# A different order of weight casts, evictions and sums where a kernel passes from plain products to block products

## The chip, the cores and the metric

One core of a Trainium2 chip runs the program. Its engines work side by side, each through a queue in program order: TensorE (PE; PEld is its weight load), VectorE (DVE), ScalarE (ACT), GpSimd (POOL) and SyncE (SP), which here only issues transfers. What counts is the device time of one execution in microseconds (us), as the median of several.

## The reference

The program computes one layer of a decoder for 512 prompt tokens and 32 sample tokens, 544 columns in all. The change lies in the first part of the feed-forward network:

```python
u = x * (1 + sc2) + sh2
h = (jax.nn.silu(u @ w_gate) * (u @ w_up)) @ w_down
x = layer_norm(DN_ALPHA * x + (1 + g2) * h, ln2_g, ln2_b)
```

`x` has 1024 channels; the hidden width is 2816, which makes 22 feature blocks of 128. Ahead of it stand the modulation, the input projection, convolution, attention, the output projection and the first layer norm, which the change leaves alone.

## The kernel before, in words

**Precision.** Each operand of a product is held as a rounded high part and a remainder. A weight tile of 128x1024 is loaded by SP into one of four raw buffers (`wr`), cast on ACT into a high part (`wh`, line 133), and DVE subtracts to get the remainder (`wl`, line 134). Three buffers each of `wh` and `wl` go round. Three products make one: high by high, high by remainder, remainder by high.

**Halves.** The 544 columns are two halves of 272. A group (`mm_group`, lines 199 to 202) multiplies one weight tile by both halves: 48 matmuls of 272 columns, into two of the four PSUM banks of `mm`. Two groups, gate and up of a feature block, are evicted together: a sigmoid on ACT and a multiply on DVE (lines 1050, 1052), a multiply by the up result (1057), a cast of the hidden value on ACT (1059) and its remainder on DVE (1061).

**The passage.** Feature blocks 0 and 1 are computed for the first half of the columns alone, then, once the layer norm of the second half is done, for the second half (lines 1307 to 1309, four other banks). So their four evictions of the first half (`first`) and of the second half (`second`) come apart. Feature blocks 2 and 3 are plain groups: gate 2, up 2, gate 3, up 3. Their weight tiles are here called by these names. Gate 2 has a buffer of its own; up 2, gate 3 and up 3 use the three round buffers, which the tiles of blocks 0 and 1 hold until the second half is done.

From block 4 on a block is computed by seven half-size products (`seven`, 12 matmuls each, 84 in all) instead of eight. The products are called by the operands of the weight: A11, S1, S2, S3, A12, A22, S4. The S operands are sums of quarter blocks: POOL makes them for the weights (line 1112, `add_up`), ACT and DVE cast and subtract them (`unit_high`, lines 1128 and 1139). The same kinds of sum of `u2`, the normed input, are made once, in the passage: ACT computes `u2` again unrounded into `tf` (line 1289, eight times), DVE makes four sums (1294, 1298 as `t3`, 1299, 1301 as `t4`), ACT casts them into `tb` and `ta` (1295, 1300, 1321, 1332) and DVE makes the remainders (1316, 1317, 1322, 1334). `ta` lies in the memory of `tf`, so its first cast waits until `tf` is read out. The weight sums `ss` lie in the memory of `t3`, so the first weight sum waits for line 1322, which reads `t3` last. A block's S4 sum overwrites its S1 sum, and the next block's S1 sum overwrites that.

**What sets the order.** Order on PE, ACT, DVE and POOL is written out by hand: an engine runs its instructions as the program text issues them, and waits where data or a buffer is not ready. `prep_to(n)` issues casts and remainders of weights up to number n, and with each a next load on SP; `w_next(k)` does so k ahead. The text of the passage is in the branch `if j == 0`.

## Time and profile before

| | us |
|---|---|
| median of 3 runs | 1026.58 (1026.53 to 1027.11) |
| the profiled execution | 1026.28 |
| its span on the chip | 1024.5 |
| the passage on PE, gate 2 to the end of up 3 | 645.06 to 678.37 |
| blocks 4 to 7 | 678.37 to 723.35 |

The granted TensorE clock was 0.993 over the span. Times in the time line count from the start of the span. A row of the time line gives the start, the length, the engine, the line, the operation and its tiles; in square brackets stands how long the engine had been idle and what ended that. In the tables a number behind x is a count of instructions. Buffer numbers are left out of names, so `wh` is any of the three.

### The profile page before, as it was taken

The numbers are of one execution on the slowest core, as the hardware profiler recorded it, in microseconds if no ns is written. First come the engines' busy times: TensorE is split into PE (matmuls) and PEld (weight loads), VectorE is DVE, ScalarE is ACT, GpSimd is POOL, SyncE is SP. The second block draws the span as 40 slices with busy tenths as digits, with TensorE's granted clock in tenths as the row PEclk, the third lists the DMA queues.
The fourth block names the chain that finished last, engine by engine and source line by source line (L and its number), as shares of the span: only waits on it lengthen the run. The fifth ranks groups of instructions, "written<-read, shape, count | busy, mean of one in ns | idle before, by whom it ended". The sixth has DMA issues, their size and how long they took to land.

```text
span 1024.5 us, 21678 instructions
## 1 busy us (share of the span) xinstructions
PE 989.5 (97%) x9000; PEld 945.6 (92%) x9000; DVE 649.0 (63%) x1165; ACT 492.5 (48%) x963; POOL 223.8 (22%) x266
## 2 busy tenths in 40 slices
PE   7999999999999999999999999899999999999994
PEld 6987899999988989999999998799999999999994
DVE  3523688879886554342216888688546875488687
ACT  3412335545447666534435745556435652356333
POOL 0201010010014310101103135054024430344046
PEclk9999999999999999999999999999999999999998
DMA  9998787796785574699943620125964769566612
GB/s 368 377 423 293 259 302 279 246 338 233 279 300 199 210 265 162 244 373 398 373 187 109 249 66 21 42 83 201 352 227 166 267 229 344 206 247 223 207 46 82
DMA packets 46529, 242.64 MB, mean 237 GB/s; under 512 B 7584, under 2 KB 12448, under 8 KB 39520
## 3 DMA queue, kind: packets, MB, share of 16 engines
q1 hardware_dynamic: 36896, 135.70, 36.8%
q10 hardware_dynamic: 7488, 87.95, 23.1%
q0 software_dynamic: 2048, 17.63, 4.4%
q8 instruction: 70, 1.15, 0.4%
q14 instruction: 27, 0.22, 0.1%
HBM read 231.36 MB, written 97.58 MB: 321 GB/s over the span
## 4 chain that ended last, share of the span: by engine, by line
PE 56%; DVE 13%; issue 10%; ACT 8%; DMA 7%; POOL 6%; ACTq 0%; SPq 0%; POOLq 0%; DVEq 0%
PE mm L199 13%; PE mm L200 13%; PE mm L202 13%; POOL ss L1112 4%; DMA gb<-in_w_ada 3%; DMA wr<-in_w_gu 2%; PE od L766 2%; PE mm L1155 2%; PE Sd L731 2%; PE mm L1157 2%; PE mm L1156 2%; DVE wl L134 1%; PE pt L542 1%; DMA wr<-in_w_in 1%; PE adaps L357 1%
## 5 line engine op out<-in xcount | busy, mean ns | idle before, releaser
L199 PE MATMUL mm<-u,wh 128*128 128x272 f32 x1016 | 284.2, 297 | 4.4 <-ACT wh L133 4.1
L200 PE MATMUL mm<-u,wh 128*128 128x272 f32 x1016 | 276.5, 290 | 0.0
L202 PE MATMUL mm<-u,wl 128*128 128x272 f32 x1016 | 213.4, 290 | 1.0 <-DVE wl L134 1.0
L199 PEld LDWEIGHTS mm<-u,wh 128*128 128x128 f32 x1016 | 192.9, 190 | 19.2 <-issue 9.8
L200 PEld LDWEIGHTS mm<-u,wh 128*128 128x128 f32 x1016 | 193.5, 190 | 0.2
L134 DVE TENSOR_TENSOR wl<-wr,wh 128x1024 fp32r<-128x1024 f32 (+2 forms) x97 | 117.2, 1209 | 82.3 <-ACT wh L133 81.3
L202 PEld LDWEIGHTS mm<-u,wl 128*128 128x128 f32 x1016 | 160.4, 189 | 1.4 <-DVE wl L134 1.4
L133 ACT CAST wh<-wr 128x1024 fp32r<-128x1024 f32 (+2 forms) x97 | 94.0, 970 | 48.5 <-PE mm L200 34.6
L465 DVE SCALAR_TENSOR_TENSOR convy<-glu,vec,convy 128x512 f32<-128x512 f32 x120 | 95.7, 797 | 2.5
L1112 POOL TENSOR_TENSOR ss<-wr 128x512 f32<-128x512 f32 x34 | 51.7, 1520 | 192.7 <-DVE s L1139 84.3
L200 PE MATMUL mm<-h,wh 128*128 128x272 f32 x240 | 64.8, 288 | 0.0
L199 PE MATMUL mm<-h,wh 128*128 128x272 f32 x240 | 64.5, 287 | 0.0
L1069 DVE SCALAR_TENSOR_TENSOR z<-mm,modT,z 128x272 f32<-128x272 f32 (+1 forms) x48 | 21.7, 479 | 50.9 <-PE mm L202 50.9
L663 ACT ACTIVATE qk<-mm,vec 128x272 f32<-128x272 f32 (+1 forms) x48 | 25.8, 624 | 53.9 <-PE mm L202 53.9
L202 PE MATMUL mm<-h,wl 128*128 128x272 f32 x240 | 49.7, 289 | 0.0
L1128 ACT CAST wh<-ss 128x512 fp32r<-128x512 f32 (+1 forms) x34 | 28.4, 835 | 42.8 <-POOL ss L1112 33.1
L199 PEld LDWEIGHTS mm<-h,wh 128*128 128x128 f32 x240 | 45.2, 188 | 0.0
L200 PEld LDWEIGHTS mm<-h,wh 128*128 128x128 f32 x240 | 45.2, 188 | 0.0
L535 ACT ACTIVATE P<-P,st 128x256 f32<-128x256 f32 x64 | 31.2, 488 | 28.3 <-DVE st L529 25.8
L1155 PE MATMUL mm<-ta,wh 128*128 128x272 f32 x136 | 40.5, 297 | 2.4 <-DVE wg L1177 2.4
L680 POOL DMA_DIRECT2D out_kv<-qk x4 | 2.4, 597 | 176.9 <-ACT qk L663 176.9
L1157 PE MATMUL mm<-tb,wl 128*128 128x272 f32 x136 | 39.5, 290 | 0.0
(342 smaller groups left out, 2547.6 us busy)
## 6 DMA issues: line engine op xcount, KB each, us to landing
out_s<-in_c ACTq DMA_DIRECT2D x32, 2044.0 KB, 9.6
wr<-in_w_in SPq DMA_DIRECT2D x57, 512.0 KB, 6.5
wr<-in_w_gu SPq DMA_DIRECT2D x44, 512.0 KB, 4.0
KT<-in_kt SPq DMA_DIRECT2D x24, 792.0 KB, 7.7
VV<-in_vv SPq DMA_DIRECT2D x24, 768.0 KB, 7.3
out_s<-in_c ACTq DMA_DIRECT2D x8, 2032.0 KB, 9.7
...
```

The source lines that it names most:

```text
L133: act.copy(out=hv, in_=raw)
L134: dve.tensor_tensor(out=lv, in0=raw, in1=hv.bitcast(F32), op=ALU.subtract)
L199: pe.matmul(ps[h][:, :HC], lhsT=hi[:, k], rhs=A[h][:, 0, k], start=(k == 0), stop=False)
L200: pe.matmul(ps[h][:, :HC], lhsT=hi[:, k], rhs=A[h][:, 1, k], start=False, stop=False)
L202: pe.matmul(ps[h][:, :HC], lhsT=lo[:, k], rhs=A[h][:, 0, k], start=False, stop=(k == nk - 1))
L465: dve.scalar_tensor_tensor(out=o, in0=src, scalar=sc, in1=o, op0=ALU.mult, op1=ALU.add)
L535: act.activation(out=p[:, a:b], in_=p[:, a:b], func=AF.Exp, bias=st[:, kd, s, hh, 0:1], accum_out=st[:, kd, s, hh, 1:2])
L663: act.activation(out=o, in_=src, func=AF.Identity, bias=V("b_in", col))
L1112: pool.tensor_tensor(out=o, in0=x, in1=y, op=op)
L1128: act.copy(out=hi, in_=src_of(f, n))
L1155: pe.matmul(ps[:, :HC], lhsT=hi[:, k], rhs=B[:, 0, k], start=(first and k == 0), stop=False, skip_group_check=not first)
L1157: pe.matmul(ps[:, :HC], lhsT=lo[:, k], rhs=B[:, 0, k], start=False, stop=(k == 3), skip_group_check=not first)
```

## The change

The four casts and remainders of up 2, gate 3, up 3 and of A11 of block 4 are issued at other places between the evictions and the `u2` sums. The second halves' sigmoids and multiplies are put ahead of their other eviction steps, in tiles of another tag. The four weight sums of block 4 are issued at the start of the passage and go to four tiles of their own (`early`); S2 and S3 of block 4 are therefore cast and subtracted one by one. PE, SP and POOL run the same instructions in the same order as before.

On ACT, at the start of the passage, before (`wr_7019` is up 2, `sgf_7581` the gate of feature block 1, first half, `tb` the `u2` sums):

```order
L1050 ACTIVATE sgf_7581<-mm_7510 128x272
L1059 CAST h00_7388<-sgf_7581 128x272
L1295 CAST tb_7564<-tf_7239 128x1088
L1289 ACTIVATE tf_7239<-z_6753,B9_6400,G9_6399 128x272 x4
L133 CAST wh_7593<-wr_7019 128x1024
L1300 CAST tb_7564<-tf_7239 128x1088
```

and in the change (`wg_7571` and `wg_7591` are the gates of feature blocks 0 and 1, `wr_7051` is gate 3):

```order
L1062 CAST h00_7388<-wg_7571 128x272
L133 CAST wh_7577<-wr_7019 128x1024
L1053 ACTIVATE wg_7591<-mm_7510 128x272
L1312 ACTIVATE tf_7239<-z_6753,B9_6400,G9_6399 128x272 x4
L1062 CAST h00_7388<-wg_7591 128x272
L133 CAST wh_7748<-wr_7051 128x1024
L1333 CAST tb_7564<-tf_7239 128x1088
```

Up 2 moved from behind the second eviction, the first `tb` cast and eight recomputations to right behind the first eviction; gate 3 stands ahead of the first `tb` cast.

On ACT, up 3 (`wr_7392`), before (`sgf_7761` and `sgf_7763` are gate 2, `wr_7051` gate 3):

```order
L1050 ACTIVATE sgf_7761<-mm_7699 128x272
L1050 ACTIVATE sgf_7763<-mm_7700 128x272
L133 CAST wh_7767<-wr_7051 128x1024
L1059 CAST h00_7388<-sgf_7761 128x272
L1059 CAST h01_7389<-sgf_7763 128x272
L1321 CAST ta_7831<-t3_7565 128x1088
L133 CAST wh_7838<-wr_7392 128x1024
```

and in the change (`wg_7755` and `wg_7757` are gate 2, `wg_7761` and `wg_7764` the second halves):

```order
L1053 ACTIVATE wg_7755<-mm_7697 128x272
L1053 ACTIVATE wg_7757<-mm_7698 128x272
L1053 ACTIVATE wg_7761<-mm_7560 128x272
L1053 ACTIVATE wg_7764<-mm_7562 128x272
L1312 ACTIVATE tf_7239<-z_6753,B9_6400,G9_6399 128x272 x4
L1062 CAST h01_7389<-wg_7761 128x272
L1062 CAST h01_7389<-wg_7764 128x272
L1341 CAST tb_7564<-tf_7239 128x1088
L133 CAST wh_7831<-wr_7392 128x1024
```

Up 3's cast no longer stands behind the eviction of feature block 2 and the cast of `ta`, but behind the second halves' evictions, four recomputations and the second `tb` cast.

On DVE, where the block products begin, before (`mm_7844` and `mm_7845` are gate 3, `mm_7910` and `mm_7911` up 3, `ss` the weight sums):

```order
L1322 TENSOR_TENSOR ta_7831<-t3_7565,ta_7831 128x1088
L134 TENSOR_TENSOR wl_7839<-wr_7392,wh_7838 128x1024
L1139 TENSOR_TENSOR wl_7895<-wr_7569,wh_7894 128x512
L1139 TENSOR_TENSOR wl_7895<-ss_7834,wh_7894 128x512
L1052 TENSOR_TENSOR sgf_7900<-sgf_7900,mm_7844 128x272
L1052 TENSOR_TENSOR sgf_7902<-sgf_7902,mm_7845 128x272
L1334 TENSOR_TENSOR ta_7831<-t4_7566,ta_7831 128x1088
L1139 TENSOR_TENSOR wl_7961<-ss_7834,wh_7960 128x1024
L1057 TENSOR_TENSOR sgf_7900<-sgf_7900,mm_7910 128x272
L1057 TENSOR_TENSOR sgf_7902<-sgf_7902,mm_7911 128x272
```

and in the change (`mm_7850` and `mm_7851` are gate 3, `mm_7912` and `mm_7913` up 3, `ss4` the weight sums of block 4):

```order
L1165 TENSOR_TENSOR wl_7847<-wr_7569,wh_7846 128x512
L1354 TENSOR_TENSOR ta_7845<-t3_7565,ta_7845 128x1088
L1165 TENSOR_TENSOR wl_7847<-ss4_7583,wh_7846 128x512
L1055 TENSOR_TENSOR wg_7905<-wg_7905,mm_7850 128x272
L1055 TENSOR_TENSOR wg_7907<-wg_7907,mm_7851 128x272
L1163 TENSOR_TENSOR wl_7963<-ss4_7585,wh_7962 128x512
L1163 TENSOR_TENSOR wl_7963<-ss4_7587,wh_7962 128x512
L1361 TENSOR_TENSOR ta_7845<-t4_7566,ta_7845 128x1088
L1060 TENSOR_TENSOR wg_7905<-wg_7905,mm_7912 128x272
L1060 TENSOR_TENSOR wg_7907<-wg_7907,mm_7913 128x272
```

The remainder of up 3 has left this piece for an earlier place, the A22 pass (line 1334, now 1361) went behind S2 and S3, and the weight sums come from tiles that do not wait for `t3`.

The diff:

```diff
@@ -1043,10 +1043,13 @@
         tick()
 
 
-    def gate_evict(pg):
+    def small(pool_, tag):
+        return pool_.tile([128, NT if tag == "w" else 512], F32, tag=tag, name="wg")[:, :HC]
+
+    def gate_evict(pg, tag="w"):
         sg = {}
         for h in pg:
-            sg[h] = tmp.tile([128, HC], F32, tag="w", name="sgf")
+            sg[h] = small(tmp, tag)
             act.activation(out=sg[h], in_=pg[h][:, :HC], func=AF.Sigmoid)
         for h in pg:
             dve.tensor_tensor(out=sg[h], in0=sg[h], in1=pg[h][:, :HC], op=ALU.mult)
@@ -1089,7 +1092,7 @@
 
 
     UNITS = ("A11", "S1", "S2", "S3", "A12", "A22", "S4")
-    rw, place, sums, T, own = {}, {}, set(), {}, {}
+    rw, place, sums, T, own, early = {}, {}, set(), {}, {}, {}
 
     def rhs_of(n):
         return T[n] if n in T else {"A11": u2[0][:, :, 0:4], "A12": u2[0][:, :, 4:8], "S4": u2[1][:, :, 4:8]}[n]
@@ -1102,6 +1105,17 @@
 
     def add_up(f, n):
         g, u = raw_of(f)
+        if f == 4:
+            e = early[f, n] = tmp4.tile([128, 4, 128], F32, tag="P", name="ss4")
+            x, y, op = {
+                "S1": (lambda: u[:, 0:4], lambda: u[:, 4:8], ALU.add),
+                "S2": (lambda: early[f, "S1"], lambda: g[:, 0:4], ALU.subtract),
+                "S3": (lambda: g[:, 0:4], lambda: u[:, 0:4], ALU.subtract),
+                "S4": (lambda: g[:, 4:8], lambda: early[f, "S2"], ALU.subtract),
+            }[n]
+            pool.tensor_tensor(out=e, in0=x(), in1=y(), op=op)
+            sums.add((f, n))
+            return
         SS = own["SS"]
         o, x, y, op = {
             "S1": (SS[:, 2], u[:, 0:4], u[:, 4:8], ALU.add),
@@ -1115,7 +1129,11 @@
     def src_of(f, n):
         g, u = raw_of(f)
         assert n[0] == "A" or (f, n) in sums
-        return {"A11": g[:, 0:4], "A12": g[:, 4:8], "A22": u[:, 4:8], "S1": own["SS"][:, 2], "S4": own["SS"][:, 2], "S2": own["SS"][:, 0:2]}[n]
+        if f == 4 and n[0] == "S":
+            return early[f, n]
+        if n[0] == "A":
+            return {"A11": g[:, 0:4], "A12": g[:, 4:8], "A22": u[:, 4:8]}[n]
+        return {"S1": own["SS"][:, 2], "S4": own["SS"][:, 2], "S2": own["SS"][:, 0:2]}[n]
 
     def unit_high(f, n, twice=False):
         j = UNITS.index(n)
@@ -1125,7 +1143,11 @@
             if j // 2 not in ring:
                 ring[j // 2] = (whp.tile([128, 8, 128], F32R, tag="wh", name="wh"), wlp.tile([128, 8, 128], F32R, tag="wl", name="wl"))
             hi, lo = (t[:, 4 * (j % 2):4 * (j % 2) + (8 if n == "S2" else 4)] for t in ring[j // 2])
-        act.copy(out=hi, in_=src_of(f, n))
+        if n == "S2" and f == 4:
+            for i, m in enumerate(("S2", "S3")):
+                act.copy(out=hi[:, 4 * i:4 * i + 4], in_=src_of(f, m))
+        else:
+            act.copy(out=hi, in_=src_of(f, n))
         if n == "S2":
             place[f, 2], place[f, 3] = (hi[:, 0:4], lo[:, 0:4]), (hi[:, 4:8], lo[:, 4:8])
         else:
@@ -1136,7 +1158,11 @@
             act.copy(out=seen, in_=f32(hi))
 
         def low():
-            dve.tensor_tensor(out=lo, in0=src_of(f, n), in1=seen, op=ALU.subtract)
+            if n == "S2" and f == 4:
+                for i, m in enumerate(("S2", "S3")):
+                    dve.tensor_tensor(out=lo[:, 4 * i:4 * i + 4], in0=src_of(f, m), in1=seen[:, 4 * i:4 * i + 4], op=ALU.subtract)
+            else:
+                dve.tensor_tensor(out=lo, in0=src_of(f, n), in1=seen, op=ALU.subtract)
             if n == "A22":
                 i = gu_at[2 * f]
                 done[i] = done[i + 1] = True
@@ -1155,9 +1181,6 @@
             pe.matmul(ps[:, :HC], lhsT=hi[:, k], rhs=B[:, 0, k], start=(first and k == 0), stop=False, skip_group_check=not first)
             pe.matmul(ps[:, :HC], lhsT=hi[:, k], rhs=B[:, 1, k], start=False, stop=False, skip_group_check=not first)
             pe.matmul(ps[:, :HC], lhsT=lo[:, k], rhs=B[:, 0, k], start=False, stop=(k == 3), skip_group_check=not first)
-
-    def small(pool_, tag):
-        return pool_.tile([128, NT if tag == "w" else 512], F32, tag=tag, name="wg")[:, :HC]
 
     rest = {}
 
@@ -1288,17 +1311,14 @@
                 for k in ks:
                     act.activation(out=tf[:, k // 4, k % 4], in_=z[:, k, :HC], func=AF.Identity, scale=G9[:, k, 0:1], bias=B9[:, k, 0:1])
 
+            f = 4
             gu_evict({0: first[0]}, {0: first[1]}, H, 0)
+            prep_to(pos["use"] + 2)
+            for n in ("S1", "S2", "S3", "S4"):
+                add_up(f, n)
+            sg = gate_evict({0: first[2]})
             again(range(4))
-            gu_evict({0: first[2]}, {0: first[3]}, H, 1)
-            dve.tensor_tensor(out=tf[:, 0], in0=tf[:, 2], in1=tf[:, 0], op=ALU.subtract)
-            act.copy(out=T["S1"][:, 0], in_=tf[:, 0])
-            again(range(4, 8))
-            prep_to(pos["use"] + 2)
-            dve.tensor_tensor(out=t3, in0=tf[:, 3], in1=tf[:, 2], op=ALU.subtract)
-            dve.tensor_tensor(out=tf[:, 3], in0=tf[:, 3], in1=tf[:, 0], op=ALU.subtract)
-            act.copy(out=T["S2"][:, 0], in_=tf[:, 3])
-            dve.tensor_tensor(out=t4, in0=tf[:, 1], in1=tf[:, 3], op=ALU.subtract)
+            up_evict(sg, {0: first[3]}, H, 1)
             A = u2[1]
             for k in range(8):
                 for i in range(4):
@@ -1308,33 +1328,38 @@
                     pe.matmul(ps, lhsT=lo[:, k], rhs=A[:, 0, k], start=False, stop=False)
                     pe.matmul(ps, lhsT=hi[:, k], rhs=A[:, 1, k], start=False, stop=(k == 7))
             pg = mm_group(w_next(2), u2, 8)
+            dve.tensor_tensor(out=tf[:, 0], in0=tf[:, 2], in1=tf[:, 0], op=ALU.subtract)
+            prep_to(pos["use"] + 2)
+            act.copy(out=T["S1"][:, 0], in_=tf[:, 0])
+            sg = gate_evict(pg)
+            sec = [gate_evict({1: second[2 * i]}, "PT") for i in range(2)]
+            again(range(4, 8))
             for i in range(2):
-                gu_evict({1: second[2 * i]}, {1: second[2 * i + 1]}, H, i)
-            sg = gate_evict(pg)
+                up_evict(sec[i], {1: second[2 * i + 1]}, H, i)
+            dve.tensor_tensor(out=t3, in0=tf[:, 3], in1=tf[:, 2], op=ALU.subtract)
+            dve.tensor_tensor(out=tf[:, 3], in0=tf[:, 3], in1=tf[:, 0], op=ALU.subtract)
+            act.copy(out=T["S2"][:, 0], in_=tf[:, 3])
+            dve.tensor_tensor(out=t4, in0=tf[:, 1], in1=tf[:, 3], op=ALU.subtract)
+            pu = mm_group(w_next(2), u2, 8)
             prep_to(pos["use"] + 2)
-            pu = mm_group(w_next(2), u2, 8)
+            up_evict(sg, pu, H, 2)
             dve.tensor_tensor(out=T["S1"][:, 1], in0=tf[:, 0], in1=f32(T["S1"][:, 0]), op=ALU.subtract)
             dve.tensor_tensor(out=T["S2"][:, 1], in0=tf[:, 3], in1=f32(T["S2"][:, 0]), op=ALU.subtract)
-            up_evict(sg, pu, H, 2)
             TA = big_tile(0, [128, 2, 2, 4, HC], F32R, "ta")
             T["S3"], T["A22"] = TA[:, 0], TA[:, 1]
+            unit_a = unit_high(f, "A11")
             act.copy(out=T["S3"][:, 0], in_=t3)
+            pg = mm_group(w_next(1), u2, 8)
+            unit_a()
             dve.tensor_tensor(out=T["S3"][:, 1], in0=t3, in1=f32(T["S3"][:, 0]), op=ALU.subtract)
             own["SS"] = one.tile([128, 3, 4, 128], F32, tag="vT", name="ss")
-            f = 4
-            for n in ("S1", "S2", "S3"):
-                add_up(f, n)
-            prep_to(pos["use"] + 2)
-            pg = mm_group(w_next(2), u2, 8)
-            unit(f, "A11")
             unit(f, "S1")
             sg = gate_evict(pg)
             act.copy(out=T["A22"][:, 0], in_=t4)
-            add_up(f, "S4")
+            pu = mm_group(w_next(1), u2, 8)
+            unit(f, "S2")
             dve.tensor_tensor(out=T["A22"][:, 1], in0=t4, in1=f32(T["A22"][:, 0]), op=ALU.subtract)
             own["S4"] = one.tile([128, 2, 4, 128], F32R, tag="osb", name="s4")
-            pu = mm_group(w_next(1), u2, 8)
-            unit(f, "S2")
             up_evict(sg, pu, H, 3)
             unit(f, "A12")
             rest["a22"] = unit_high(f, "A22")
```

## The prediction

> **What bounds the kernel now.** I read the page first, then the busy time in stretches around the place of the change, then the time line of TensorE (PE), VectorE (DVE), ScalarE (ACT) and GpSimd (POOL) there. The page says that PE has work nearly all the time:
>
> ```profile
> PE 989.5 (97%) x9000; PEld 945.6 (92%) x9000; DVE 649.0 (63%) x1165; ACT 492.5 (48%) x963; POOL 223.8 (22%) x266
> ```
>
> So a gain must come out of stretches in which PE waits or is slow. The table of stretches (start:end, length, busy time of PE, PEld, DVE, ACT, POOL with instruction counts, granted PE clock, DMA share, GB/s) is cut where each piece of the passage starts on PE: gate 2, up 2, gate 3, up 3, then the blocks 4, 5, 6 and 7 of seven products.
>
> ```profile
> 645.06:651.11 6.05, 6.05 (x50) 5.97 (x48) 2.52 (x4) 3.23 (x7) 0.00 (x0) 1.00 0.00 1
> 651.11:661.95 10.84, 8.06 (x50) 7.63 (x48) 7.12 (x9) 4.87 (x10) 0.00 (x0) 0.84 0.16 48
> 661.95:672.35 10.40, 8.07 (x51) 7.70 (x50) 8.96 (x13) 4.91 (x9) 1.25 (x1) 0.84 0.18 53
> 672.35:678.37 6.02, 6.02 (x51) 6.02 (x50) 5.89 (x6) 3.24 (x5) 5.94 (x4) 1.00 0.30 87
> 678.37:690.87 12.50, 10.85 (x87) 10.63 (x85) 9.60 (x16) 7.31 (x14) 6.07 (x5) 1.00 0.29 85
> 690.87:701.93 11.06, 10.84 (x86) 10.62 (x85) 8.68 (x18) 6.65 (x13) 5.47 (x4) 1.00 0.76 274
> 701.93:712.77 10.84, 10.84 (x87) 10.63 (x85) 8.65 (x18) 6.62 (x13) 5.47 (x4) 1.00 0.36 108
> 712.77:723.35 10.58, 10.58 (x86) 10.58 (x85) 8.63 (x17) 4.25 (x8) 0.00 (x0) 1.00 0.80 290
> ```
>
> Without a wait a group of 48 matmuls takes 6.05 us (0.126 each) and a block of 84 takes 10.58. Against that, up 2 loses 4.79, gate 3 4.35, block 4 1.92, block 5 0.48 and block 6 0.26: 11.80 us in all, which no reordering here can exceed. PE's own rows say what it waited for:
>
> ```profile
> 653.54 0.40 PE L199 MATMUL mm<-u,wh 128*128 128x272 f32 x1 [2.29 <-ACT wh L133]
> 654.80 0.52 PE L202 MATMUL mm<-u,wl 128*128 128x272 f32 x2 [0.49 <-DVE wl L134]
> 663.94 0.39 PE L199 MATMUL mm<-u,wh 128*128 128x272 f32 x1 [1.83 <-ACT wh L133]
> 665.20 0.65 PE L202 MATMUL mm<-u,wl 128*128 128x272 f32 x2 [0.49 <-DVE wl L134]
> 687.75 0.39 PE L1155 MATMUL mm<-ta,wh 128*128 128x272 f32 x1 [1.65 <-DVE wg L1177]
> ```
>
> In both weight stages PE waits for the rounding cast on ACT (wh) and then for its remainder on DVE (wl): 2.78 and 2.32 us. What is left of 4.79 and 4.35, 2.0 each, is the clock: it was 0.84 in both stretches. Why is up 2's cast late? It is not the transfer:
>
> ```profile
> 649.42 1.10 ACT L1295 CAST tb<-tf 128x1088 fp32r<-128x1088 f32 x1 [1.77 <-DVE tf L1294]
> 650.43 2.12 ACT L1289 ACTIVATE tf<-z,B,G 128x272 f32<-128x272 f32 x4
> 652.46 1.03 ACT L133 CAST wh<-wr 128x1024 fp32r<-128x1024 f32 x1
> 653.52 1.23 DVE L134 TENSOR_TENSOR wl<-wr,wh 128x1024 fp32r<-128x1024 f32 x1 [4.19 <-ACT wh L133]
> ```
>
> On ACT's queue the cast of up 2 stands behind the S1 sum's cast and four recomputations of u2, and DVE then sits 4.19 us with nothing. Gate 3's cast is late likewise, behind eight evictions that go back and forth between ACT and DVE.
>
> **The change, part by part.** PE, SP and POOL keep their order; ACT and DVE change. I replay the new order by hand with these durations: a 128x1088 pass on DVE 1.29, its cast on ACT 1.10, a sigmoid 0.39, an eviction's multiply, cast and remainder 0.44, 0.42, 0.44; a weight's cast 1.03 and remainder 1.23; four recomputations 2.12 (the last two from above). Independent operations follow each other about 0.08 sooner.
>
> ```profile
> 655.98 1.29 DVE L1299 TENSOR_TENSOR tf<-tf 128x1088 f32<-128x1088 f32 x1
> 659.28 0.44 DVE L1057 TENSOR_TENSOR sgf<-sgf,mm 128x272 f32<-128x272 f32 x1
> 660.20 0.44 DVE L1061 TENSOR_TENSOR h<-sgf,h 128x272 fp32r<-128x272 f32 x1 [0.49 <-ACT h L1059]
> 657.31 1.10 ACT L1300 CAST tb<-tf 128x1088 fp32r<-128x1088 f32 x1 [3.82 <-DVE tf L1299]
> 658.32 0.39 ACT L1050 ACTIVATE sgf<-mm 128x272 f32<-128x272 f32 x1
> 659.75 0.42 ACT L1059 CAST h<-sgf 128x272 fp32r<-128x272 f32 x1 [1.05 <-DVE sgf L1057]
> ```
>
> *Up 2.* Its cast now follows the first eviction. It needs the buffer of gate 0, which PE's last round over the second halves frees about 0.9 us before 645.06. Cast 644.2 to 645.2, remainder to 646.5; PE asks at 651.1. The banks that it writes are read out by 647.4. Gain 4.79, hidden behind gate 2's 6.05.
>
> *Gate 3.* Sigmoid and four recomputations end at 647.6, the eviction's cast at 648.0, gate 3's cast at 649.0, the S1 sum on DVE at 649.6, gate 3's remainder at 650.8; PE asks at 657.2. Gain 4.35.
>
> *Up 3* becomes the late one. From PE's end of gate 2 at 651.1: four sigmoids to 652.6 (gate 2 and, early, the second halves), four recomputations to 654.6, then cast, remainder, multiply, cast and remainder of the second halves to 656.95; on DVE t3 to 658.25 and the S2 sum to 659.55; on ACT its cast to 660.6 and up 3's cast to 661.65; remainder to 662.9. PE asks at 663.2. But its banks are those of up 2, whose multiplies stand behind that remainder: free at 663.25 and 663.6. PE loses 0.3.
>
> *Block 4 starts.* Its bank is gate 3's. Before the multiply that frees it DVE has two remainders of up 2's eviction (to 664.5), two S1/S2 passes (to 666.9), the A11 remainder, the S3 pass, which waits for its cast on ACT because the tile reuses the sums' memory (cast to 668.1, pass to 669.4), and the S1 remainder (to 669.9). The multiply ends at 670.3, PE is free at 669.6: loses 0.7.
>
> *The weight sums* go to temporaries of their own and need no tile of t3's memory; they can run once up 4 lands. Its load is issued when up 2's remainder frees a buffer (646.5) and takes 4.0:
>
> ```profile
> wr<-in_w_gu SPq DMA_DIRECT2D x44, 512.0 KB, 4.0
> ```
>
> So the four sums run from 650.5 to 655.6, where DVE mostly reads PSUM. That matters, since sums and DVE passes whose two inputs lie in SBUF exclude each other. First POOL's four sums, then DVE in the same microseconds, then one remainder and one sum that ran alone:
>
> ```profile
> 671.11 2.20 POOL L1112 TENSOR_TENSOR ss<-wr 128x512 f32<-128x512 f32 x1 [31.74 <-DVE ta L1322]
> 673.38 1.63 POOL L1112 TENSOR_TENSOR ss<-ss,wr 128x512 f32<-128x512 f32 x1
> 674.98 1.74 POOL L1112 TENSOR_TENSOR ss<-wr 128x512 f32<-128x512 f32 x1
> 676.68 2.33 POOL L1112 TENSOR_TENSOR ss<-wr,ss 128x512 f32<-128x512 f32 x1
> 672.08 1.78 DVE L1139 TENSOR_TENSOR wl<-wr,wh 128x512 fp32r<-128x512 f32 x1
> 673.99 1.57 DVE L1139 TENSOR_TENSOR wl<-ss,wh 128x512 fp32r<-128x512 f32 x1
> 676.18 1.68 DVE L1334 TENSOR_TENSOR ta<-t,ta 128x1088 fp32r<-128x1088 f32 x1
> 677.84 2.26 DVE L1139 TENSOR_TENSOR wl<-ss,wh 128x1024 fp32r<-128x1024 f32 x1
> 682.84 0.69 DVE L1139 TENSOR_TENSOR s<-ss,s 128x512 fp32r<-128x512 f32 x1 [0.35 <-ACT s L1128]
> 685.36 1.28 POOL L1112 TENSOR_TENSOR ss<-ss,wr 128x512 f32<-128x512 f32 x1
> ```
>
> Remainders of 0.69, 0.69, 1.29 and 1.23 took 1.78, 1.57, 1.68 and 2.26: 1.09, 0.88, 0.39 and 1.03 more, each ending one pass after a sum ends; they take turns. The collision of block 4's sums disappears, but block 5's three sums, which now wait only for the S3 pass (669.4) and up 5's load (issued 662.9), fall on block 4's S2, S3 and A22 remainders. I price that at the mean, 0.85 x 3 = 2.5. The bounds are nothing and 3 x 1.28 = 3.8.
>
> The Trainium skill, page "SBUF — State Buffer", section "SBUF: two separate sides", says that the shared port pair is an exclusive lock held for the whole instruction, so that the loser fully blocks. By that rule three collisions can cost DVE up to the 3.8 us, and the sum below would end at 1022.3. The rows agree with the taking of turns, but show a mean of 0.85, since a pass mostly meets a sum half done.
>
> *Block 4 runs.* After 669.9 DVE has two multiplies, S2, S3 (0.6 each) and A22 (1.2): 673.0 free of collisions, 675.5 with them. Then come up 3's multiplies, which free the bank of the third product; PE asks at 673.4, so it stalls 2.6. How long from there to the sixth product, the one that waited 1.65 above? Before:
>
> ```profile
> 680.02 0.77 DVE L1057 TENSOR_TENSOR sgf<-sgf,mm 128x272 f32<-128x272 f32 x2
> 685.32 0.62 ACT L1128 CAST wh<-ss 128x512 fp32r<-128x512 f32 x1 [1.08 <-POOL ss L1112]
> ```
>
> From 680.02 to 687.75 it was 7.73, of which ACT spent 1.08 waiting for block 5's S1 sum. That sum is now done early: 6.65. So the sixth product starts at 675.5 + 6.65 = 682.15 and block 5 3.12 later (687.75 to 690.87), at 685.3. Before it was 690.87: **5.6 us less**. One more cast and one more remainder (S2 and S3 apart) cost 0.1 each and lie in that chain, which makes it 5.5. Blocks 5 and 6 keep their 0.48 and 0.26, for there POOL's S1 sum waits for the S4 remainder as it did.
>
> The profiled execution took 1026.28 (span 1024.5 and 1.8 around it), 0.3 below the median of 1026.58. 1026.28 - 5.5 is 1020.8; against the median 1021.1. I predict **1021.0**. The shift reaches the end: after 723.35 PE waits for no transfer, only for DVE, 0.9 us in all, most of it here:
>
> ```profile
> PE mm L1155 <- DVE wg L1177: 0.6, 3, 0.2
> ```
>
>
> **The rivals.** *A, the sum above*: own range 1019.6 to 1022.5.
>
> *B, the sums of block 5 miss DVE* (DVE wins the turns, or POOL comes later). Up 3's multiplies start at 673.0, the third product does not wait, and 2.5 more are gained: 1018.5. For it: the load could land late. Against it: the strict turns above.
>
> *C, the sums of block 4 fall on up 3's chain.* If up 4 lands 3 us late, they meet the second halves' remainders, t3, the S2 sum and up 3's remainder, all with both inputs in SBUF: 1.09 + 0.88 + 0.39 + 1.03 = 3.4 later on a chain with 0.3 of slack. PE then waits over 3 us for up 3, but what follows hangs on DVE, so block 5 shifts by 3.4: 1024.4. Against it: the transfers there share the engines with little (DMA share 0.16).
>
> *D, the waits only move.* ACT and DVE must still do the same work; if their handing to and fro fills what was idle, block 5 starts as before: 1026.6. For it: three stalls remain on PE in my replay. Against it: DVE's idle 4.19 in one piece, which the new order fills.
>
> *E, slower: the clock stays low.* The third product's wait of 2.6 is about as long as the two that were followed by 0.84. At the low clock matmuls start 0.22 apart:
>
> ```profile
> 655.57 0.43 PE L199 MATMUL mm<-u,wh 128*128 128x272 f32 x1
> 655.79 0.43 PE L200 MATMUL mm<-u,wh 128*128 128x272 f32 x1
> ```
>
> If one low period follows another from 676.1 on, 60 matmuls of block 4 end at 689.6 instead of 685.3 and block 5 takes 19.0, to 708.6, where it ended at 701.93: 6.7 slower, 1033. Each matmul at the low clock costs 0.1, so it is slower than before by the measurable 2 us once the low clock lasts through some 30 matmuls of block 5. Against it: both low periods above ended by themselves under a dense stream.
>
> The page "TensorE: Matmul & The Clock Gate" of the Trainium skill, section "Why this matters for your kernels", wants idle gaps of more than about 3 us before the clock falls. By it E could not start and gate 3's gap would have cost no clock; the trace disagrees, with 0.84 after 1.83 and 0.49 us of waiting.
>
> **How the numbers follow.** A 0.62, B 0.12, C 0.13, D 0.06, E 0.07. A measurement of this kernel tells 0.2%, 2.05 us, from no change. A, B and half of C (2.2 gained) are faster: 0.81. D and the other half of C are the same: 0.12. E is slower: 0.07. For the range I take in B and C, 1018.4 to 1024.5, and leave out D, E and the tails.
>
> **What would show it.** Right: up 2 and gate 3 take 6.05 each at clock 1.00; POOL's first four sums lie near 650 to 656; PE's waits are for up 3's bank (below 1), for block 4's first bank (below 1) and for the third product (2 to 3); block 5 starts near 685.3. Wrong: a wait for a weight cast that remains; block 5's sums that do not lengthen S2, S3 and A22 (B); up 3 at 666 or later (C); a clock under 1.00 beyond block 4 (E); or a stretch after 723 that got longer by what was gained.

## The result, and the profile after

The changed kernel took 1021.51 us (median of four, 1021.33 to 1022.8). The kernel before, timed beside it, took 1026.84. The ratio is 0.9948, with a 95% interval of 0.9937 to 0.996: 5.3 us faster, where 5.5 was forecast. A second set gave 1021.94 against 1027.11, ratio 0.9949 (0.9937 to 0.9962).

The profiled execution of the changed kernel is the slowest of the four (1022.8). Its page shows the same work for PE in a shorter span, 1020.8:

```profile
PE 989.5 (97%) x9000; PEld 946.2 (93%) x9000; DVE 651.2 (64%) x1166; ACT 492.8 (48%) x964; POOL 220.1 (22%) x266
```

The table of stretches of the changed kernel has the columns of the one in the prediction, and again begins with gate 2, up 2, gate 3 and up 3; the last four rows are the blocks 4 to 7:

```profile
646.75:652.77 6.02, 6.02 (x50) 6.02 (x49) 4.79 (x6) 4.80 (x9) 1.08 (x1) 1.00 0.28 87
652.77:658.79 6.02, 6.02 (x50) 6.02 (x49) 3.68 (x8) 4.00 (x10) 4.47 (x4) 1.00 0.26 87
658.79:665.27 6.48, 6.18 (x51) 5.99 (x49) 5.61 (x7) 2.17 (x3) 0.00 (x0) 1.00 0.01 3
665.27:672.33 7.06, 6.29 (x49) 6.08 (x49) 6.30 (x10) 4.61 (x9) 0.93 (x1) 1.00 0.28 75
672.33:687.44 15.11, 12.55 (x84) 12.14 (x85) 13.93 (x20) 8.16 (x16) 5.33 (x4) 0.89 0.23 70
687.44:698.16 10.72, 10.72 (x86) 10.63 (x85) 8.33 (x17) 6.67 (x13) 5.48 (x4) 1.00 0.78 295
698.16:708.99 10.83, 10.83 (x86) 10.63 (x85) 8.63 (x18) 6.63 (x13) 5.47 (x4) 1.00 0.31 97
708.99:719.58 10.59, 10.59 (x86) 10.59 (x85) 8.63 (x17) 4.26 (x8) 0.00 (x0) 1.00 0.77 282
```

Up 2 and gate 3 fell from 10.84 and 10.40 to 6.02 and 6.48, up 3 grew from 6.02 to 7.06, and block 4 from 12.50 to 15.11. From gate 2 to block 7 it is 62.24 us (708.99 - 646.75); before it was 67.71 (712.77 - 645.06). That is 5.47 less. What was gained at up 2 and gate 3 (8.74) is 3.3 more than that; up 3 and block 4 took it back (1.04 and 2.61, less 0.4 elsewhere).

The start of gate 2 itself lies 1.69 later than before in this execution. 1.07 of that is a stretch of low clock ahead of the passage, in code that the change leaves alone; it stands in some of the profiles of this study and not in others (last section). Gate 2 starts between 645.0 and 647.5 in them, with the changed kernel alone at 646.75 and 646.35. So the experiments below are compared by medians, and inside a profile by the distance from gate 2's start. Only one execution of each set has a profile, and what is read in a profile need not hold for the median of its set.

These are the three waits of the changed PE in the passage and in block 4, in its time line:

```profile
665.27 0.37 PE L199 MATMUL mm<-u,wh 128*128 128x272 f32 x1 [0.29 <-DVE wg L1060]
672.33 0.39 PE L1181 MATMUL mm<-u,wh 128*128 128x272 f32 x1 [0.77 <-DVE wg L1055]
678.09 0.57 PE L1181 MATMUL mm<-tb,wh 128*128 128x272 f32 x1 [2.48 <-DVE wg L1060]
```

They are up 3's bank, block 4's first bank and the bank of the third product. The sixth product shows no wait here; why not is told at rival E. Why the third waits 2.48 stands in the rows of POOL and DVE of the changed kernel:

```profile
671.40 1.67 POOL L1126 TENSOR_TENSOR ss<-wr 128x512 f32<-128x512 f32 x1 [14.08 <-DVE ta L1354]
673.15 1.62 POOL L1126 TENSOR_TENSOR ss<-ss,wr 128x512 f32<-128x512 f32 x1
674.73 1.71 POOL L1126 TENSOR_TENSOR ss<-wr 128x512 f32<-128x512 f32 x1
672.64 2.68 DVE L1163 TENSOR_TENSOR wl<-ss,wh 128x512 fp32r<-128x512 f32 x2
675.24 2.35 DVE L1361 TENSOR_TENSOR ta<-t,ta 128x1088 fp32r<-128x1088 f32 x1
677.52 0.77 DVE L1060 TENSOR_TENSOR wg<-wg,mm 128x272 f32<-128x272 f32 x2
```

POOL's three sums of block 5 start as soon as `ta`'s S3 pass has read `t3`, and run into S2, S3 and A22 on DVE. Those take 2.68 and 2.35; alone they take 1.29 and 1.29 (rows of a run below). The collision costs 2.45, and up 3's multiplies, which free the bank, stand right behind.

### The profile page after: what moved, and what is told of

The parts are those of the page before. It is cut to its first block, busy times and chain, and to the rows that moved or that the text cites. A ratio compares the mean times of both kernels' runs of the same rounds, so it can differ in the third digit from the quotient of the medians.

```text
span 1020.8 us, 21673 instructions
## 1 busy us (share of the span) xinstructions
PE 989.5 (97%) x9000; PEld 946.2 (93%) x9000; DVE 651.2 (64%) x1166; ACT 492.8 (48%) x964; POOL 220.1 (22%) x266
## 4 chain that ended last, share of the span: by engine, by line
PE 64%; DVE 11%; issue 7%; DMA 7%; ACT 6%; POOL 4%; ACTq 0%; POOLq 0%; DVEq 0%; SPq 0%
PE mm L199 15%; PE mm L200 14%; PE mm L202 14%; POOL ss L1126 4%; DMA gb<-in_w_ada 3%; PE mm L1181 2%; DMA wr<-in_w_gu 2%; PE mm L1183 2%; PE mm L1182 2%; PE od L766 2%; PE Sd L731 2%; PE pt L542 1%; DVE wl L134 1%; PE o L558 1%; PE adaps L357 1%
## 5 line engine op out<-in xcount | busy, mean ns | idle before, releaser
L1126 POOL TENSOR_TENSOR ss<-wr 128x512 f32<-128x512 f32 x32 | 47.2, 1476 | 171.8 <-DVE s L1165 79.7
L1181 PE MATMUL mm<-tb,wh 128*128 128x272 f32 x136 | 40.0, 294 | 2.5 <-DVE wg L1060 2.5
```

What stands on the lines that cost most here:

```text
L1126: pool.tensor_tensor(out=o, in0=x, in1=y, op=op)
L1181: pe.matmul(ps[:, :HC], lhsT=hi[:, k], rhs=B[:, 0, k], start=(first and k == 0), stop=False, skip_group_check=not first)
```

## The experiments

Two accounts of the result stood against each other. **P**, stall by stall: each wait of PE that goes is a gain and each new one a loss. The list of stalls in the prediction (4.79, 4.35, 1.92, ...) reads like that. **Q**, the chain: what decides is one chain of passes on ACT and DVE, from PE's end of gate 2 to the sixth product of block 4; PE's waits ahead of that are slack and show only where the chain's lead was spent. The prediction's last steps, which replay ACT and DVE up to block 5, are of that kind. As a sum afterwards P is always right, since PE's span is its work and its waits; the question is whether one wait can be priced beforehand, as if the others stayed. On the change itself both give much the same. Four kernels were timed beside a kernel before of 1027.05 (the first four below), four beside 1027.11 (block 5's sums held back, the A22 pass later, up 3 earlier, and the change again), three beside 1027.05 and the last beside 1026.92.

### Weight sums back in the memory of t3

The change without its own temporaries for block 4's weight sums (S2 and S3 of block 4 are cast and subtracted in one pass again):

```diff
-            for n in ("S1", "S2", "S3", "S4"):
-                add_up(f, n)
             sg = gate_evict({0: first[2]})
...
             own["SS"] = one.tile([128, 3, 4, 128], F32, tag="vT", name="ss")
+            for n in ("S1", "S2", "S3"):
+                add_up(f, n)
             unit(f, "S1")
+            add_up(f, "S4")
             sg = gate_evict(pg)
```

> The change without the temporaries: block 4's four weight sums lie in t3's memory again and wait for the S3 pass; casts and evictions in the new order. Two theories stand against each other in these runs. Q: one chain of passes on DVE and ACT decides; it begins when PE ends gate 2 and leads to the sixth product of block 4. What counts is when that chain may run on and what is put into it; PE's waits for up 2 and gate 3 and the low clock lie beside it and cost nothing of their own. P: PE's losses add up, each stall is worth its size. Q: the sums wait for the S3 pass and take turns with S1, A22 and S2 on DVE, and block 5's S1 sum waits for the S4 remainder again, so about 2.2 of the gain is lost: about 3.6 faster than before, 0.9965. If the casts alone bring the gain: 5.3 faster, 0.9948. P: up 2 and gate 3 stay cured, 9.1, minus new stalls as large as in the change, so again about 5 faster.

Measured: 1024.08, ratio 0.997 (0.9958 to 0.9981), 3.0 us faster than before and so 2.3 short of the change. Q's 3.6 lies inside the interval (2.0 to 4.3), P's 5 and the 5.3 of the casts alone do not. PE's waits in this run:

```profile
672.56 0.59 PE L1160 MATMUL mm<-u,wh 128*128 128x272 f32 x1 [3.25 <-DVE wg L1055]
677.32 0.37 PE L1160 MATMUL mm<-tb,wh 128*128 128x272 f32 x1 [0.21 <-DVE wg L1060]
684.48 0.39 PE L1160 MATMUL mm<-ta,wh 128*128 128x272 f32 x1 [2.37 <-DVE wg L1179]
```

The third product waits 0.21 here, not 2.48, and yet the kernel is slower: block 4's first product waits 3.25, because the S1 remainder stands ahead of the multiply that frees its bank and now waits for POOL, and the sixth waits 2.37. The sixth product starts 39.40 behind gate 2 (684.48 - 645.08), 1.83 later than in the change (37.57), where Q had the loss at 1.7. The other 1.5 by which block 5 comes later in this profile is clock: products six and seven took 4.65 at a granted clock of 0.63, against 3.12 at 1.00.

### Own temporaries alone

The kernel before, with the four weight sums issued early into own tiles, and so S2 and S3 of block 4 cast and subtracted apart; the order of the rest stays:

```diff
             prep_to(pos["use"] + 2)
+            for n in ("S1", "S2", "S3", "S4"):
+                add_up(f, n)
...
-            for n in ("S1", "S2", "S3"):
-                add_up(f, n)
...
             act.copy(out=T["A22"][:, 0], in_=t4)
-            add_up(f, "S4")
```

> Only the temporaries: the order of before for casts and evictions, block 4's sums in four tiles of their own, issued behind up 2's cast. Q: up 4 lands near 658.5, the sums take turns with the evictions (gate 3 about 1 later), but S1, A22 and S2 run free of them and block 5's S1 sum is early, so block 5 starts 1.3 earlier and block 5 loses less: about 2.0 faster, 0.998. P: only block 4's own loss of 1.92 can go, at most 1.9 faster, and 1 of it is given back at gate 3: 0.9 faster, 0.999. If the two parts only work together: no change, 1.000.

Measured: 1026.22, ratio 0.9989 (0.998 to 0.9998), 0.8 us less in the medians; from gate 2 to block 7 the profile has 66.24 for 67.71, 1.47 less. P's 0.9 is met here, and Q's 2.0 lies at the edge of the interval (0.2 to 2.05), so by itself this run speaks for P rather than for Q. In its profile block 5 starts 45.07 behind gate 2 (690.37 - 645.30), 0.74 sooner than before (45.81), where Q had 1.3. The same temporaries are worth 2.3 in the change and about 1 here, because here the sums meet other passes. In POOL's and DVE's rows of this run:

```profile
660.02 1.30 POOL L1113 TENSOR_TENSOR ss<-ss,wr 128x512 f32<-128x512 f32 x1
...
660.41 1.21 DVE L1061 TENSOR_TENSOR h<-sgf,h 128x272 fp32r<-128x272 f32 x1 [0.49 <-ACT h L1059]
...
662.99 1.28 DVE L1061 TENSOR_TENSOR h<-sgf,h 128x272 fp32r<-128x272 f32 x1 [0.48 <-ACT h L1059]
```

The two remainders of the second halves take 1.21 and 1.28 where they took 0.44, and gate 3's cast stands behind them: PE waits 3.45 for it instead of 1.83. So the parts of the change do not seem to add up by themselves, though the intervals of the two differences are wide.

### The cast of up 2 alone

The kernel before, with one step moved: up 2's cast and remainder right behind the first eviction.

```diff
             gu_evict({0: first[0]}, {0: first[1]}, H, 0)
+            prep_to(pos["use"] + 2)
             again(range(4))
...
             again(range(4, 8))
-            prep_to(pos["use"] + 2)
             dve.tensor_tensor(out=t3, in0=tf[:, 3], in1=tf[:, 2], op=ALU.subtract)
```

> Only up 2's cast and remainder are moved to right behind the first eviction; all else as before. PE's wait at up 2 goes, with its low clock: up 2 takes 6.05 instead of 10.84. P: 4.8 faster, 0.9953. Q: gate 3's cast still stands behind the same evictions and keeps its time to within 0.6, so PE waits there 4 to 6 us instead of 2, and block 5 starts only 0.6 earlier: 0.6 faster, 0.9994.

Measured: 1023.47, ratio 0.9967 (0.9955 to 0.998): 3.6 us faster (2.05 to 4.6). Both accounts missed, P's 4.8 by little and Q's 0.6 by far. The stretches up 2 and gate 3 of this run:

```profile
652.64:661.88 9.24, 6.19 (x51) 5.97 (x49) 6.63 (x12) 6.76 (x13) 0.00 (x0) 0.98 0.00 0
661.88:671.00 9.12, 9.12 (x48) 8.82 (x49) 8.43 (x10) 3.23 (x5) 1.97 (x1) 0.65 0.16 60
```

Up 2 itself no longer waits, but gate 3 now waits 3.05 for its cast (in the first row) and then runs at a clock of 0.65. So part of P's 4.8 came back at gate 3. For Q a link of the chain had been set wrong, which was found only after this result: I had taken `t3` and the S2 sum to wait for the second four recomputations. They don't, as DVE's rows of this run show:

```profile
652.05 1.29 DVE L1298 TENSOR_TENSOR t<-tf 128x1088 f32<-128x1088 f32 x1
653.37 1.29 DVE L1299 TENSOR_TENSOR tf<-tf 128x1088 f32<-128x1088 f32 x1
655.39 1.29 DVE L1301 TENSOR_TENSOR t<-tf 128x1088 f32<-128x1088 f32 x1 [0.73 <-ACT tf L1289]
```

Only the third of these, `t4`, waits for them (0.73). In the kernel before, `t3` and the S2 sum stood behind up 2's remainder on DVE's queue; with the remainder gone ahead, counted from gate 2's start (646.62 here, 645.06 there), `t3` comes 5.43 behind it instead of 9.60, the evictions that follow on DVE 10.06 (656.68) instead of 13.68 (658.74), and gate 3's cast on ACT 14.16 (660.78) instead of 17.79 (662.85), 3.6 sooner. Block 7 then comes 64.10 behind gate 2 instead of 67.71, 3.6 sooner as well: what the chain gained in the evictions it kept to the end.

### The two waits filled with work

The kernel before, with 18 matmuls ahead of up 2 and 30 ahead of gate 3 (6.0 us at 0.126), which use an older weight and which nothing reads:

```diff
+        for _ in range(fill[0]):
+            pe.matmul((ps[0] if fill[2] is None else fill[2])[:, :HC], lhsT=fill[1][:, 0], rhs=A[0][:, 0, 0], start=True, stop=True)
...
-            pu = mm_group(w_next(2), u2, 8)
+            wu2 = w_next(2)
+            pu = mm_group(wu2, u2, 8, fill=(18, wg2[0], None))
...
-            pg = mm_group(w_next(2), u2, 8)
+            pg = mm_group(w_next(2), u2, 8, fill=(30, wu2[0], ps_s.tile([128, 512], F32, tag="s", name="fill")))
```

> The kernel before, with matmuls that nothing reads put into PE's two waits: 18 ahead of up 2 and 30 ahead of gate 3, so that PE does not go idle there. The waits for the casts stay, the low clock behind them should go (1.00 instead of 0.84 in both stretches). P, with 2.0 us for the clock in each: 2 to 4 faster, 0.996 to 0.998. Q: up 2 and gate 3 end 2 us earlier each, but what follows them waits for the same casts and multiplies, and the sixth product of block 4 starts when it did: no change, 1.000.

Measured: 1027.03, ratio 0.9999 (0.999 to 1.0008). The rows of up 2 and gate 3:

```profile
651.30:661.90 10.60, 10.10 (x79) 9.66 (x78) 7.11 (x9) 4.63 (x10) 0.00 (x0) 1.00 0.16 51
661.90:672.30 10.40, 9.57 (x75) 9.12 (x73) 8.59 (x12) 5.28 (x9) 0.87 (x1) 1.00 0.17 51
```

The clock is 1.00 where it was 0.84, and the stretches are hardly shorter (10.84 and 10.40 before): from gate 2 (645.41) to block 7 (713.05) it is 67.64, and was 67.71. The sixth product of block 4 starts 42.65 behind gate 2, 42.69 before, and PE waits 2.17 for it instead of 1.65. So the 2.0 us that the prediction put down to the clock in each stage had no price of their own: PE at full clock only waits longer for the next pass.

### Three microseconds of PE work put into the change

The most direct test of P: the changed kernel, with 24 unread matmuls ahead of up 2.

```diff
-            pu = mm_group(w_next(2), u2, 8)
+            pu = mm_group(w_next(2), u2, 8, fill=(24, wg2[0]))
```

> The change, and PE does 24 matmuls of 272 columns more (3.0 us at 0.126) ahead of up 2, into up 2's first bank, whose own first matmul starts afresh, so that nothing reads them. This puts back most of what PE lost at up 2 before the change, on PE alone. Theory P (each wait of PE counts): 3.0 us slower than the change, ratio 0.9978. Theory Q (the chain of DVE and ACT passes from PE's end of gate 2 to the sixth product of block 4 decides): gate 3, up 3 and block 4's first product start 3.0, 2.9 and 1.8 later, the third product and all behind it as before: the time of the change, ratio 0.9949 within 0.4 us.

Measured: 1022.09, ratio 0.9948 (0.9935 to 0.9962), the time of the change. The filler, and then the stretch up 2 with the filler, that of products three to five of block 4, and PE's two waits in this block:

```profile
652.24 3.18 PE L198 MATMUL mm<-u,h 128*128 128x272 f32 x24
```

```profile
652.24:661.30 9.06, 9.06 (x75) 9.06 (x74) 6.65 (x11) 4.33 (x11) 4.50 (x4) 1.00 0.19 60
677.61:683.85 6.24, 4.77 (x37) 4.55 (x37) 5.08 (x11) 5.95 (x13) 0.26 (x1) 1.00 0.41 110
677.61 0.36 PE L1183 MATMUL mm<-tb,wh 128*128 128x272 f32 x1 [1.11 <-DVE wg L1062]
683.85 0.39 PE L1183 MATMUL mm<-ta,wh 128*128 128x272 f32 x1 [1.46 <-DVE wg L1202]
```

Up 2 is 3.0 longer. Up 3's wait of 0.29 and block 4's of 0.77 are gone, and the third product's fell from 2.48 to 1.11. In place of it PE waits 1.46 for the sixth product: products three to five run at a clock of 1.00 here, and ran at 0.75 in the change. The sixth product starts 37.62 behind gate 2 (683.85 and 646.23), in the change run again 37.56, and block 7 62.30, in the change 62.24. So P is refuted for up 2 and gate 3: up to some 3 us of PE's time there have no price, filled into the waits of the kernel before or put back into the change.

### Block 5's sums held back

The change, with a tiny POOL operation that reads up 3's multiply, ahead of block 5's first sums. This tests rival B.

```diff
             up_evict(sg, pu, H, 3)
+            hold = const.tile([128, 32], F32, name="hold")
+            pool.tensor_tensor(out=hold, in0=sg[1][:, :32], in1=sg[1][:, :32], op=ALU.add)
             unit(f, "A12")
```

> The change, but block 5's first weight sums are held back until up 3's multiplies, so that they no longer collide with the S2, S3 and A22 passes of block 4 on DVE. Theory P (each of PE's waits is a loss of its own): the third product's wait of 2.5 us goes, and with it 2.5 us of the time: ratio 0.9924. Theory Q (the chain of DVE and ACT passes up to the sixth product of block 4 decides): the same sums now meet the passes that follow, up to the sixth product; the third product waits for less than 0.3 us, the sixth for about 2, and the time is that of the change, ratio 0.9948 within 0.5 us.

Measured: 1023.24, ratio 0.9959 (0.9945 to 0.9972), 1.3 slower than the change beside it (0.9949), though the intervals overlap. The collision did go from S2, S3 and A22, and came back one step on; DVE's rows of this run:

```profile
672.16 1.29 DVE L1163 TENSOR_TENSOR wl<-ss,wh 128x512 fp32r<-128x512 f32 x2
673.37 1.29 DVE L1361 TENSOR_TENSOR ta<-t,ta 128x1088 fp32r<-128x1088 f32 x1
...
675.50 1.93 DVE L1064 TENSOR_TENSOR h<-wg,h 128x272 fp32r<-128x272 f32 x2
677.35 1.78 DVE L1165 TENSOR_TENSOR wl<-wr,wh 128x512 fp32r<-128x512 f32 x1
679.05 1.77 DVE L1165 TENSOR_TENSOR s<-ss,s 128x512 fp32r<-128x512 f32 x1
```

1.93 for two remainders of up 3's eviction was 0.79, and 1.78 and 1.77 were 0.69 each. PE's third product does not wait; the sixth waits 3.18:

```profile
683.88 0.40 PE L1181 MATMUL mm<-ta,wh 128*128 128x272 f32 x1 [3.18 <-DVE wg L1200]
```

It starts 37.60 behind gate 2 (646.28), and 37.56 in the change beside it (683.91 - 646.35). So Q is right to 0.04 us on the sixth product, and B's 2.5 do not come: at this other place on the chain the sums cost as much. Q's time, that of the change within 0.5 us, is missed all the same. In this profile block 5 starts 1.58 later behind gate 2 than in the change beside it (42.25 against 40.67), of which blocks 5 and 6 give back 0.38. That comes behind the sixth product, from a place that neither account had:

```profile
683.88:688.53 4.65, 4.64 (x24) 4.65 (x25) 3.86 (x6) 1.59 (x4) 1.03 (x1) 0.63 0.16 58
```

The sixth and seventh product took 4.65 at a granted clock of 0.63; in the change they took 3.11 at 1.00.

### The A22 pass later

The change, with the A22 pass behind up 3's eviction instead of ahead of it:

```diff
             unit(f, "S2")
-            dve.tensor_tensor(out=T["A22"][:, 1], in0=t4, in1=f32(T["A22"][:, 0]), op=ALU.subtract)
-            own["S4"] = one.tile([128, 2, 4, 128], F32R, tag="osb", name="s4")
             up_evict(sg, pu, H, 3)
+            dve.tensor_tensor(out=T["A22"][:, 1], in0=t4, in1=f32(T["A22"][:, 0]), op=ALU.subtract)
+            own["S4"] = one.tile([128, 2, 4, 128], F32R, tag="osb", name="s4")
```

> The change, but the A22 pass of ta on DVE stands behind up 3's eviction instead of ahead of it. Theory Q: the third product of block 4 waits 0.5 us instead of 2.5, the sixth product, which needs that pass, waits about 0.5; block 5 starts 1.85 us sooner than in the change: ratio 0.993 (1019.7 us). Theory P: the third product's wait of 2.5 goes but for the two passes of 0.6 that stay ahead, 2.0 less: ratio 0.9929. The two agree here; the run is a candidate for a faster kernel.

Measured: 1021.53, ratio 0.9943 (0.9931 to 0.9956), 0.4 better than the change and inside its interval; the five times reach from 1019.77 to 1022.62. The profile, of the slowest of the five, shows products three to five and then six and seven:

```profile
675.97:683.23 7.26, 5.03 (x36) 4.59 (x36) 6.36 (x12) 6.05 (x13) 0.91 (x2) 1.00 0.32 90
683.23:687.76 4.53, 4.53 (x25) 4.53 (x26) 3.86 (x6) 1.59 (x4) 1.03 (x1) 0.65 0.30 102
```

The sixth product starts 36.31 behind gate 2 (646.92), 1.25 sooner than in the change (1.85 was expected for block 5). PE had waited 1.91 for it (0.5 was expected), and 0.20 for the third. Then the two products take 4.53 at a clock of 0.65, 1.42 more than 3.11, and the gain is gone in this execution. Both accounts had a ratio of about 0.993, which lies just outside the interval. The other four executions have no profile, so whether the clock took the gain in the median too is not shown.

### Up 3 earlier as well

The kernel of the last experiment, with up 3's cast and remainder ahead of the second four recomputations and the second halves' further eviction:

```diff
             sec = [gate_evict({1: second[2 * i]}, "PT") for i in range(2)]
+            prep_to(pos["use"] + 3)
             again(range(4, 8))
```

> As the kernel before it, and up 3's cast and remainder are also moved ahead, behind the sigmoids and multiplies of the second halves and ahead of the second four recomputations. Theory Q: the chain gets shorter ahead of up 3's multiplies, since its remainder (1.23 us) leaves the place between the S2 sum and the eviction of up 2; but there it meets block 4's weight sums and takes 2.3. Block 5 starts 2.7 us sooner than in the change: ratio 0.9921 (1018.8 us), 0.9 better than the kernel without it. Theory P: only up 3's wait of 0.3 is saved: 0.2 to 0.3 better than the kernel without it.

Measured: 1018.94 (1018.57 to 1021.22), ratio 0.9928 (0.9915 to 0.994): 3.0 faster than the change beside it, 8.2 faster than before. It beats both kernels. From gate 2 to block 7 it takes 59.95, 2.28 less than the change beside it (62.23). Its stretches of products three to five and of six and seven:

```profile
673.52:680.78 7.26, 5.04 (x36) 4.60 (x36) 6.36 (x12) 6.05 (x13) 0.92 (x2) 1.00 0.32 91
680.78:683.90 3.12, 3.12 (x25) 3.12 (x25) 3.12 (x5) 1.21 (x3) 1.03 (x1) 1.00 0.32 130
```

P expected 0.2 to 0.3 over the kernel without the step, Q 0.9; measured were 2.6 in the medians, with intervals that just overlap. Inside the profiles the sixth product comes 1.03 sooner behind gate 2 (35.28 against 36.31), which is Q's 0.9; block 5 comes 2.44 sooner (38.40 against 40.84), and the other 1.41 is the clock, which here was 1.00 in products six and seven, after a wait of 1.90. How much of the 2.6 between the medians is clock is not shown.

### Filling the wait for the sixth product

Three tries to keep the clock up with unread matmuls between the fifth and the sixth product of block 4. The first two, on the last two kernels, read the weight of the fifth product:

```diff
+        w5 = place[f, 4][0]
         product(f, 4, X, False)
...
+        if f == 4:
+            fill = ps_t.tile([128, 512], F32, tag="t", name="fill")[:, :HC]
+            for _ in range(14):
+                pe.matmul(fill, lhsT=w5[:, 0], rhs=u2[0][:, 0, 4], start=True, stop=True)
         product(f, 5, Zc, False)
```

> As the kernel with the A22 pass later and up 3 earlier, and PE does 14 matmuls (1.76 us) that nothing reads while it waits 1.90 us for the sixth product of block 4. Theory Q with the clock's part: such a wait costs a second time where a low-clock period follows it, since behind the sixth product PE itself is the end of the chain; in the profile of this kernel none fell there, but two of its five times were 1.3 and 2.3 us above the others. Filled, the time is that of its faster runs: 1018.7 us, ratio 0.992, and no run above 1019.5. Theory that a filled wait changes nothing: 1018.9 with the same spread.

> As the kernel with the A22 pass later alone, and the same 14 matmuls in the wait of 1.91 us ahead of the sixth product of block 4. Without them the sixth and seventh product took 4.53 us at a granted clock of 0.65 where 3.11 is usual. Theory Q with the clock's part: these two take 3.1 us, block 5 starts 1.4 us sooner, 1020.0 us, ratio 0.9932. Theory that a filled wait changes nothing, as in the run with filled waits ahead of up 2 and gate 3: 1021.5, ratio 0.9943.

Measured: 1021.73, ratio 0.9952 (0.9939 to 0.9964), and 1023.95, ratio 0.9971 (0.9959 to 0.9982): 2.8 and 2.4 slower than the same kernels unfilled. The filler of the second one:

```profile
684.41 2.62 PE L1256 MATMUL fill<-u,wh 128*128 128x272 f32 x14 [2.54 <-ACT wh L1150]
```

It did not run in the wait but began when that was over. The tile of the fifth product's weight is used again for block 5, and its next cast on ACT (683.75 to 684.36) was issued ahead of the filler; so the filler reads what that cast writes, and waits for it. As tests of the clock both failed; behind their fillers products six and seven ran at 0.70 and 0.73. As tests of the chain they say something else: PE's sixth product came 2.9 and 3.1 later behind gate 2, and here, unlike at up 2, PE's delay counts: 2.8 and 2.4 in the medians, of which the low clock behind the fillers may be a part.

The third try, on the kernel with the A22 pass later alone, takes an operand that is long there:

```diff
         product(f, 4, X, False)
+        if f == 4:
+            fill = ps_t.tile([128, 512], F32, tag="t", name="fill")[:, :HC]
+            for _ in range(13):
+                pe.matmul(fill, lhsT=u2[0][:, 0, 4, :128], rhs=u2[0][:, 0, 4], start=True, stop=True)
```

> The kernel with the A22 pass later alone, and 13 matmuls (1.64 us) that nothing reads right behind the fifth product of block 4, with an operand that has long been there, so that they start at once and end within the wait of 1.91 us for the sixth product. In the kernels filled there before, they read a tile that a later cast on ACT overwrites and so started 2.4 us too late, at the end of that cast. Theory that the low clock costs time there: the sixth and seventh product take 3.1 us instead of 4.53, block 5 starts 1.4 us sooner: 1020.1 us, ratio 0.9932. Theory that a filled wait changes nothing: 1021.5, ratio 0.9943.

Measured: 1021.51 (1020.76 to 1021.74), ratio 0.9944 (0.9931 to 0.9958): the time unfilled, 1021.53, with less spread. The filler, and products six and seven:

```profile
682.26 1.90 PE L1249 MATMUL fill<-u 128*128 128x272 f32 x13 [1.56 <-DVE wl L1165]
```

```profile
684.00:687.01 3.01, 3.01 (x26) 3.01 (x25) 2.57 (x5) 0.96 (x2) 0.00 (x0) 1.00 0.12 24
```

The filler waited again, 1.56, this time for a remainder on DVE. That remainder reads `hip`, and the kernel's text gives `hip` and the filler the same bank: both are tiles of `ps_t` with tag `t`, which has one buffer (lines 70 and 1157 of the changed kernel). So the sixth product starts 37.71 behind gate 2 (646.29) instead of 36.31, 1.4 late. But behind the filler the clock is 1.00 and the two products take 3.01, not 4.53. The one ate the other: block 5 starts 40.72 behind gate 2, and 40.84 unfilled. That the filler kept the clock up is not shown: the kernel with up 3 earlier had 1.00 there without one, and the two fillers above were followed by a low clock. What a filler that starts in time would bring was not measured.

## Why the prediction was right, point by point

**The total.** 5.5 forecast; 5.3 in the medians, 5.47 from gate 2 to block 7. Block 5 was to start 40.24 behind gate 2 (685.3 - 645.06); it starts 40.69 behind. Of the 0.45 too little, 0.35 came back in blocks 5 and 6, which were to keep their waits of 0.48 and 0.26 and so their 21.90 together, and took 21.55: block 5 came down to 10.72, 0.14 over 10.58. That was not forecast, so the last few tenths of the agreement are luck.

**The steps on PE.** Up 2 6.02 (6.05 forecast). Gate 3's own matmuls likewise, up 3's bank 0.29 (0.3). Block 4's first bank 0.77 (0.7). Third product 2.48 (2.6), from a collision of 2.45 (0.85 x 3 = 2.5). The S2, S3 and A22 passes lost 1.39 and 1.06, so the mean from the rows held, and not the upper bound of 3.8; the rows behind the mean reach from 0.39 to 1.09, so that it came out to 0.05 is partly luck. From up 3's multiplies to the sixth product 6.80 (677.52 to 684.32; 6.65 forecast).

**Rival C** came in small. Three of POOL's four sums of block 4 ran off the chain as forecast. The fourth fell on a remainder of the second halves, which is on it:

```profile
656.03 1.29 POOL L1116 TENSOR_TENSOR ss<-wr,ss 128x512 f32<-128x512 f32 x1
656.45 1.17 DVE L1064 TENSOR_TENSOR h<-wg,h 128x272 fp32r<-128x272 f32 x1 [1.35 <-ACT h L1062]
```

The remainder took 0.44 in the run with the sums in the memory of `t3`, whose order on DVE is the same up to there, so it lost 0.73. The prediction's own times had this overlap (sums to 655.6, the remainder from about 655.0) and put no price on it. It hardly shows in the total: up 3's remainder starts 16.80 behind gate 2, where the replay had 16.59. That C at its full size, with up 4's load 3 us late, costs 3.4 was not tested.

**What was wrong in it**, though it did not enter the number: the working began with stalls of PE, "Gain 4.79" and "Gain 4.35", of which 2.0 each were to be the clock. The runs show that none of these is a price by itself. Filled waits at full clock changed nothing (0.9999), and 3.0 us of PE work put back at up 2 changed nothing (0.9948). What the change gained it gained on the chain: from gate 2 to the sixth product DVE was busy for 31.78 of 42.69 us before and for 31.20 of 37.57 after, so 4.54 of the 5.12 gained there is idle time of DVE that went, first of all the 4.19 in which it stood behind up 2's cast (3.6 with that cast alone moved). The number came out because its last steps replayed that chain to block 5.

Its list of PE's waits was one short. By its own times the fifth product ends about 680.5 (676.0 and 36 matmuls of 0.126) and the sixth starts at 682.15, which is a wait of some 1.6. The profile seemed to bear the short list out, because a low clock filled that time.

**Rival B** was given 1018.5 for the case that block 5's sums miss DVE's three passes. They were made to miss them by coming later, and the time was 1023.24; that DVE wins the turns was not tested. Its step "Up 3's multiplies start at 673.0, the third product does not wait, and 2.5 more are gained" failed at the sixth product, which then waits 3.18. The price was counted up to the next wait, not to the end of the chain.

**Rival E** had the right resource and the wrong place. The low periods in these profiles end by themselves, but one that falls on the sixth and seventh product costs 1.4 to 1.5, since PE is the chain there. In the profile of the change the clock was 0.89 over block 4, but products six and seven took 3.12 (684.32 to 687.44). It fell ahead of them, on products three to five (0.75), which took 6.23 instead of 4.54. This pass frees the sixth product's bank:

```profile
683.83 0.43 DVE L1200 TENSOR_TENSOR wg<-wg,mm 128x272 f32<-128x272 f32 x1
```

It ends at 684.26 and the product starts at 684.32, so PE at full clock would have waited there. In the run with 24 matmuls ahead of up 2 it had full clock at this place, and waited 1.46.

**D** is out: block 5 did not start as before.
